# State-space layer of a two-layer diffusion backbone: the scaled x is split one or two chunks ahead of its state product, the decays begin four chunks ahead, and their tile is parted in two

## The chip, the core and the metric

The kernel runs on one core of a Trainium2 chip. TensorE (PE in the profile) multiplies matrices into accumulator banks (PSUM); VectorE (DVE), ScalarE (ACT) and GpSimd (POOL) work elementwise, POOL on the working memory (SBUF) alone; SyncE (SP) issues nearly all transfers (DMAs). Each engine works through its own queue in order and waits at the head of it. The metric is the time of one execution in microseconds (us) as the device gives it.

## The reference, cut to what matters

One inference step goes through an even layer and then an odd layer, for 128 context tokens and 1024 latent tokens, which makes nine chunks of 128 tokens; chunk 0 is the context. The odd layer (attention) is not touched. The even layer holds a bidirectional state-space scan (Mamba-2 SSD) beside a pooling branch. The scan has 16 heads of width 64 in 4 groups, state size 128, and for one direction it computes

```python
a = chunk(dt * A)                                  # dt > 0, A < 0
a_cs = jnp.cumsum(a, axis=2)
l_mat = exp(where(lower, a_cs[l] - a_cs[s], -inf)) # decay from token s to token l in a chunk
cb = einsum('bclgn,bcsgn->bcgls', Cc, Bc)
y_diag = einsum('bcgrls,bcsgrp->bclgrp', cb * l_mat, xdt)
decay_to_end = exp(a_cs[:, :, -1:] - a_cs)
states = einsum('bclgn,bclgr,bclgrp->bcgrpn', Bc, decay_to_end, xdt)
h = h * exp(a_cs[:, :, -1]) + states               # from chunk to chunk
y_off = einsum('bclgn,bcgrpn,bclgr->bclgrp', Cc, h_prev, exp(a_cs))
y = y_diag + y_off
```

The second direction does the same on the flipped sequence; both results and `x * D` are summed. The context's final state of each direction is an output too. Matrix products must be nearly as exact as in 32 bits.

## The kernel before, in words

A 32-bit operand of a matrix product is split in two 16-bit halves: ACT rounds it to the first (`split`, line 510), and POOL, or DVE where none is named, subtracts that from the operand to get the second (line 511). A product is then three matmuls (`mm3`, lines 330 to 332): high by high, high by low, low by high. Since these lines are a helper's, the profile tells products apart by their tiles: `xshl` is the split of the scaled x, `hb` and `hf` that of the backward and forward states, `E` the decays (and, later, the masked product), `psss` an accumulator bank of the state-space stage (four of them, taken in turn).

The scan runs group by group (`ssd_group`, `ssd_steps`, g = 0 to 3). For one group:

- Contexts (`context`, line 788): the state product of chunk 0 for both directions, scaled by ACT (line 791) and stored. In odd groups they come before the state pass, in even groups in the first step of the output pass.
- State pass (line 841): for one direction, chunk by chunk, the state before the chunk is split into `hb`, and seven steps carry it on. A step (`step`, line 775) takes x of the chunk in 32 bits (`x32`, line 758, the sum of its two halves, here on POOL), multiplies it on DVE by the decay to the chunk's end (line 767, tile `xs`, two buffers), splits it on ACT and POOL (tile `xshl`, two buffers), multiplies B by it on PE, and adds the product to the decayed state on DVE (line 780). The decayed state is made on POOL (line 778).
- Output pass (line 868): for each of the nine chunks, the other direction's state is carried along with the same step, here with x32 on DVE; `y` starts as x times the diagonal term on POOL (line 875); the masked product times x is added to it (lines 893 and 895), and the two states' part (lines 901 to 906).
- `decay(c)` (line 794) prepares the mask of a chunk, for both directions in one tile `E` of 1024 columns, five buffers (`NE`): a DMA brings the cumulated decays of both directions to all partitions (line 798, 512 KB); then for each of four heads ACT adds one bias (line 801), DVE takes the minimum with the other direction (line 802) and ACT writes the dt factors over the second half (line 804); an exponential on ACT (line 806) and a multiply on POOL (line 807) end it.
- `prep(c)` (line 812) multiplies B and C of the chunk on PE into a bank, takes the diagonal from it on DVE (lines 819 and 821), multiplies the mask by the bank on DVE (line 825), and splits the result on ACT and POOL. The two 16-bit halves, `M`, are written over the second half of the same tile, so that one buffer is held from the DMA to the output product.

In the text, decays of the first three chunks stand in steps 0, 2 and 4 of the state pass (`DECAY_AT`), preps of two in steps 5 and 6; in the output pass chunk n has the decay of chunk n + 3 and the prep of chunk n + 2.

PE's instructions keep the order of the text. Between the steps, `yield` hands the order to a filler (`Filler`, line 72), which puts in as many matmuls of projections and of the pooling branch as the yielded share says: `FILL` over the sum of shares (`STORE`, `OUT_A`, `OUT_B`, `CONTEXT`, `LEAD`) is the number of estimated microseconds for one share. The elementwise work of the filler (convolutions, gates, weight splits at lines 323 and 324) goes to the same queues. The order within the queues of DVE, ACT, POOL and SP isn't that of the text: a scheduler fixes it when the program is built, by priorities, by when its model has operands ready, and by when buffers are free. The scan's steps have the higher priority; the loads of weights (line 313) do too.

Of the kernel before, what the change touches and what calls it, by code (L numbers as in the profile page):

```python
# [10 lines left out]
F32 = mybir.dt.float32  # L11
F16 = mybir.dt.float16
I32 = mybir.dt.int32
AF = mybir.ActivationFunctionType
# [27 lines left out]
STORE, OUT_A, OUT_B, CONTEXT = 1.0, 0.5, 0.5, 0.75  # L42
DECAY_AT, PREP_AT = (0, 2, 4), (5, 6)
ADA_EVERY = 4.5
# [4 lines left out]
SCORE_BANKS = ("S1", "s4", "S1", "m3", "S1")  # L49
NE = 5  # L50

# [170 lines left out]
class Builder:  # L222
# [518 lines left out]
    def ssd_steps(self, g):  # L741
# [13 lines left out]
        def v3(x):  # L755
            return x.rearrange("p (a b) -> p a b", a=4)

        def x32(c, eng=nc.vector):
            x = self.wt([P, 256], F32, tag="x32", bufs=2)
            xk = self.xb[d1, c // 3][0]  # L760
            eng.tensor_tensor(x.rearrange("p (a b) -> p a b", a=2), xk[:, :, 0, c % 3], xk[:, :, 1, c % 3], ALU.add)
            return x

        def state(c, d, x):

            xs = self.wt([P, 256], F32, tag="xs", bufs=2)
            nc.vector.tensor_tensor(v3(xs), v3(x), hcol(self.dec, c, d), ALU.mult)
            hl = self.wt([P, 2, 256], F16, tag="xshl", bufs=2)
            self.split(hl, xs, nc.gpsimd)
            st = self.pt("ss")[:, :256]  # L770
            bk = self.xb[d1, c // 3][1]
            self.mm3(st, bk[:, 0, c % 3], bk[:, 1, c % 3], hl[:, 0], hl[:, 1], True, True)
            return st

        def step(h, c, d, x):

            hn = self.wt([P, 256], F32, tag="hst", bufs=2)
            nc.gpsimd.tensor_tensor(v3(hn), v3(h), hcol(self.etot, c, d), ALU.mult)
            st = state(c, d, x)
            nc.vector.scalar_tensor_tensor(hn, st, IWS, hn, ALU.mult, ALU.add)  # L780
            return hn
# [6 lines left out]
        def context(x, d):  # L788

            so = self.wt([P, 256], F32, tag="xs", bufs=2)  # L790
            nc.scalar.activation(so, state(0, d, x), AF.Copy, scale=IWS)
            nc.sync.dma_start(self.O["ssd"][d, :, g * 256:(g + 1) * 256], so)

        def decay(c):

            ef = self.wt([P, 1024], F32, tag="E", bufs=NE)
            E = ef.rearrange("p (a b c) -> p a b c", a=2, b=4)
            nc.sync.dma_start(ef, self.csrow[g, c].rearrange("d h l -> (d h l)").partition_broadcast(P))
            for hh in range(4):
                i = g * 4 + hh  # L800
                nc.scalar.activation(E[:, 0, hh], E[:, 0, hh], AF.Identity, bias=self.cs[:, c, i:i + 1])
                nc.vector.scalar_tensor_tensor(E[:, 0, hh], E[:, 1, hh], self.cs[:, c, 16 + i:17 + i], E[:, 0, hh],
                                               ALU.add, ALU.min)
                nc.scalar.activation(E[:, 1, hh], self.tri[:, 0], AF.Identity, bias=self.dt[:, c, 16 + i:17 + i],
                                     scale=self.dtd[:, c, i:i + 1])
            nc.scalar.activation(E[:, 0], E[:, 0], AF.Exp)
            nc.gpsimd.tensor_tensor(E[:, 0], E[:, 0], E[:, 1], ALU.mult)
            Es[c] = ef

        Es, dgs = {}, {}  # L810

        def prep(c):

            ef = Es.pop(c)
            cb = self.pt("ss")[:, :P]
# [7 lines left out]
            dgs[c] = dgt[:, 0:4]  # L823
            S = ef[:, :512].rearrange("p (a b) -> p a b", a=4)
            nc.vector.tensor_tensor(S, S, cb.rearrange("p (a b) -> p a b", a=1).broadcast_to([P, 4, P]), ALU.mult)
            M = ef[:, 512:].bitcast(F16).rearrange("p (x a b) -> p x a b", x=2, a=4)
            self.split(M, S, nc.gpsimd)
            return M

        yield LEAD[g]  # L830
        order = range(NCH) if d1 == 0 else range(NCH - 1, -1, -1)
# [7 lines left out]
        Ms = {}  # L839
        scan = range(1, 9) if d0 == 0 else range(8, 0, -1)  # L840
        for n, c in enumerate(scan):
            self.split(hb[:, c - 1], h, nc.gpsimd)
            if n == 7:
                break
            h = step(h, c, d0, x32(c, nc.gpsimd))
            if n in DECAY_AT:
# [16 lines left out]
        carry(scan[0], h)  # L863
        x = x32(order[0])
        if d1:
            h = step(h, scan[0], d1, x)
            carry(scan[1], h)
        for n, c in enumerate(order):
            if n + 3 < NCH:
                decay(order[n + 3])  # L870
            if n + 2 < NCH:
                Ms[order[n + 2]] = prep(order[n + 2])
            yield OUT_A

            nc.gpsimd.tensor_tensor(v3(y[:, c]), v3(x), dgs.pop(c).rearrange("p (a b) -> p a b", b=1).broadcast_to([P, 4, 64]),
                                    ALU.mult)
# [5 lines left out]
            if n + 1 < NCH:  # L882
                e = order[n + 1]
                x = x32(e)
                if e in scan[:7]:
                    h = step(h, e, d1, x)
                    carry(scan[scan.index(e) + 1], h)
# [754 lines left out]
```

## Time and profile before

| what | value |
|---|---|
| median of 3 runs | 2299.93 us (2294.38 to 2300.79) |
| the profiled execution | 2299.1 us |
| its span, first to last instruction | 2297.3 us |
| PE, DVE, ACT, POOL busy in the span | 2031.8, 1534.2, 1293.6, 1067.8 us |
| mean granted TensorE clock | 0.954 of full |
| loads of the decays (tile E) | 36, 512 KB each, 3.9 us to landing (median) |
| loads of even-layer weights (tile w from in_wev) | 40, 512 KB each, 4.0 us to landing (median) |

How its lines are read. In a table of waits, "A line <- B line: t, n, m" says that engine A stood idle t us in total, in n waits, of which the longest took m, before its instruction of that line, and that B's instruction ended those waits. In a row of a tile, the three numbers behind the count are the shortest, the median and the longest duration in nanoseconds, followed by the first and the last start in us. In a table of windows, each engine has its busy time and its number of instructions, and behind them stand the granted clock, the share of the DMA engines' time, and the rate in GB/s; a table of one line's instructions has that line's engine alone. Busy time includes time in which an instruction was held up after its start.

### The profile page before, as it was taken

What the parts mean: (1) busy time and instruction counts of PE and PEld (TensorE: products, weight loads), DVE (VectorE), ACT (ScalarE), POOL (GpSimd) and SP (SyncE); (2) the same over time, 40 slices, a digit from 0 to 9 for tenths busy, and PEclk for the clock granted to TensorE, in tenths of its full rate; (3) what the DMA queues carried; (4) which work ended last, traced back from release to release, by engine and by line L of the source; (5) the groups of instructions that cost most, each with busy time, mean ns of one, the idle gap of its engine ahead of it and who ended that gap; (6) DMA issues with size and microseconds to landing.
All of it is one profiled execution on the core that took longest, in us unless ns stands there. A gap on an engine that the chain in (4) does not pass through costs nothing. (4 is left out here: it accounts for less than half of the span.)

```text
span 2297.3 us, 50851 instructions
## 1 busy us (share of the span) xinstructions
PE 2031.8 (88%) x20258; PEld 1452.5 (63%) x20258; DVE 1534.2 (67%) x3329; ACT 1293.6 (56%) x3530; POOL 1067.8 (46%) x997
## 2 busy tenths in 40 slices
PE   4997788787999999978898998988977999898997
PEld 2654475564557555656686676775766777686566
DVE  5868989789585444747877777778785545552334
ACT  5575666666363311436666666666676777773321
POOL 1378677876674100134445445345345656552001
PEclk9998899998999999999999999999999999999999
DMA  7221514224657522135555455544556786899412
GB/s 275 70 80 50 147 58 111 82 80 131 222 184 209 174 71 86 40 102 114 97 125 115 96 113 116 105 107 105 105 124 133 151 168 143 171 180 205 155 47 83
DMA packets 434990, 283.17 MB, mean 123 GB/s; under 512 B 374432, under 2 KB 385216, under 8 KB 434752
## 3 DMA queue, kind: packets, MB, share of 16 engines
q1 hardware_dynamic: 433776, 279.34, 49.7%
q8 instruction: 158, 2.59, 0.5%
q10 hardware_dynamic: 976, 0.58, 0.1%
q14 instruction: 80, 0.66, 0.1%
HBM read 133.38 MB, written 29.05 MB: 71 GB/s over the span
## 5 line engine op out<-in xcount | busy, mean ns | idle before, releaser
L330 PE MATMUL psmm<-h,whl 128*128 128x384 f16 (+1 forms) x1104 | 369.9, 336 | 16.7 <-DVE q L1171 11.5
L331 PE MATMUL psmm<-h,whl 128*128 128x384 f16 (+1 forms) x1104 | 368.7, 335 | 2.3 <-DVE h L507 1.7
L332 PE MATMUL psmm<-h,whl 128*128 128x384 f16 (+1 forms) x1104 | 368.7, 335 | 0.0
L330 PE MATMUL psmm<-whl,h 128*128 128x128 f16 x1920 | 345.9, 224 | 0.0
L331 PE MATMUL psmm<-whl,h 128*128 128x128 f16 x1920 | 345.7, 224 | 0.0
L332 PE MATMUL psmm<-whl,h 128*128 128x128 f16 x1920 | 345.4, 224 | 0.0
L330 PEld LDWEIGHTS <-whl 128*128 128x128 f16 x2256 | 226.6, 100 | 162.0 <-issue 23.6
L332 PEld LDWEIGHTS <-whl 128*128 128x128 f16 x2256 | 225.4, 100 | 157.1 <-issue 18.6
L331 PEld LDWEIGHTS <-whl 128*128 128x128 f16 x2256 | 225.9, 100 | 151.6 <-issue 27.6
L1307 POOL TENSOR_TENSOR phl<-p,phl 128x1152 f16<-128x1152 f32 (+1 forms) x72 | 159.9, 2221 | 249.8 <-ACT phl L1306 210.2
L330 PEld LDWEIGHTS <-h 128*128 128x128 f16 x2520 | 250.9, 100 | 9.4 <-issue 3.8
L331 PEld LDWEIGHTS <-h 128*128 128x128 f16 x2520 | 250.8, 100 | 6.9 <-issue 1.2
L332 PEld LDWEIGHTS <-h 128*128 128x128 f16 x2520 | 250.8, 100 | 0.0
L324 DVE SCALAR_TENSOR_TENSOR whl<-w,whl 128x512 f16<-128x512 f32 x248 | 191.0, 790 | 67.6 <-ACT whl L323 67.1
L1385 POOL TENSOR_TENSOR phl<-p,phl 128x1024 f16<-128x1024 f32 (+2 forms) x72 | 135.0, 1876 | 117.6 <-ACT phl L1384 117.2
L323 ACT ACTIVATE whl<-w 128x512 f16<-128x512 f32 x248 | 140.6, 609 | 78.8 <-PE psmm L332 42.3
L1289 ACT ACTIVATE p<-psS,sms 128x384 f32<-128x384 f32 (+1 forms) x240 | 136.0, 569 | 66.0 <-DVE sms L1286 65.6
L1174 POOL TENSOR_TENSOR sw<-sw,sin 128x384 f32<-128x384 f32 (+1 forms) x78 | 87.4, 1121 | 154.2 <-DVE sw L1173 126.4
L1303 DVE SCALAR_TENSOR_TENSOR p<-p,sms,p 128x384 f32<-128x384 f32 (+1 forms) x200 | 151.9, 793 | 2.5
L1282 DVE TENSOR_REDUCE mx<-psS 128x1 f32<-128x384 f32 (+1 forms) x240 | 125.2, 540 | 37.4 <-PE psS L1280 37.4
L1280 PEld LDWEIGHTS <-Q 128*128 128x128 f16 x800 | 73.7, 98 | 117.6 <-issue 82.4
L504 POOL TENSOR_TENSOR h<-mt,h 128x384 f16<-128x384 f32 (+2 forms) x32 | 29.1, 919 | 252.8 <-ACT h L503 252.8
(396 smaller groups left out, 6122.8 us busy)
## 6 DMA issues: line engine op xcount, KB each, us to landing
w<-in_wod SPq DMA_DIRECT2D x52, 512.0 KB, 3.7
w<-in_wev SPq DMA_DIRECT2D x40, 512.0 KB, 4.0
E<-csrow SPq DMA_DIRECT2D x36, 512.0 KB, 3.9
Q<-qhl SPq DMA_DIRECT2D x64, 288.0 KB, 4.6
go_dr<-gl SPq DMA_DIRECT2D x15, 576.0 KB, 3.3
wada<-in_w_ada SPq DMA_DIRECT2D x32, 256.0 KB, 5.4
o<-in_w_ada SPq DMA_DIRECT2D x16, 512.0 KB, 5.8
xT<-in_w_ada SPq DMA_DIRECT2D x16, 512.0 KB, 6.5
```

Source lines behind the costliest of these rows:

```text
L323: nc.scalar.activation(hl[:, 0, a:e], w[:, a:e], AF.Copy if scale is None else AF.Identity, scale=sc)
L324: nc.vector.scalar_tensor_tensor(hl[:, 1, a:e], w[:, a:e], sc, hl[:, 0, a:e], ALU.mult, ALU.subtract)
L330: mm(out, ah, bh, start=start, stop=False)
L331: mm(out, ah, bl, start=False, stop=False)
L332: mm(out, al, bh, start=False, stop=stop)
L1174: nc.gpsimd.tensor_tensor(sw[:, o:], sw[:, o:], self.sinT[:, a:b], ALU.mult)
L1280: nc.tensor.matmul(sv, q[:, m, x, qs], k[:, m, o + c0:o + c1], start=x == 0, stop=x == 1)
L1282: nc.vector.tensor_reduce(out=mx[:, j:j + 1], in_=sv, axis=AX.X, op=ALU.max)
L1289: nc.scalar.activation(pm[:, c0:c1], ss[j], AF.Exp, bias=nb, accum_out=sm[:, i:i + 1])
L1303: nc.vector.scalar_tensor_tensor(p[0][:, c0:c1], p[1][:, c0:c1], sm[:, 2:3], p[0][:, c0:c1], ALU.mult, ALU.add)
L1307: nc.gpsimd.tensor_tensor(phl[:, w:2 * w], p[0][:, :w], phl[:, :w], ALU.subtract)
L1385: nc.gpsimd.tensor_tensor(phl[:, 2 * w:4 * w], p, phl[:, :2 * w], ALU.subtract)
```

## The change

- `state` is parted. `scaled(c, d, x)` does the scaling and the split and returns the halves; `state(c, hl)` does the product alone. `step` takes the halves.
- In the state pass, the first chunk's x is summed, scaled and split before the first yield of the group, and each further one ahead of the step before it. In the output pass, `ahead(n)` sums x of the n-th chunk of the order, and scales and splits it where that chunk has a state step; it is called for chunks 0 and 1 ahead of the loop, and for chunk n + 2 in chunk n, behind its prep.
- The contexts scale and split where they did.
- `x32` and `xshl` have three buffers instead of two; `xs` keeps two.
- The decay's tile becomes two tiles of 512 columns, each with its own DMA of half the size: `E0` (tag E, four buffers), which is free once prep has split it, and `E1` (tag EM, six buffers), which takes the second direction, then the dt factors, then the halves `M`. Together they take the room of the five before.
- Decays stand at steps 0, 2, 3 and 5 of the state pass, four instead of three, and in the output pass one chunk further ahead, n + 4.

The products on PE, their order, and the number of elementwise instructions are the same.

```diff
-DECAY_AT, PREP_AT = (0, 2, 4), (5, 6)
+DECAY_AT, PREP_AT = (0, 2, 3, 5), (5, 6)
...
-NE = 5
+NE0, NE1 = 4, 6
...
-            x = self.wt([P, 256], F32, tag="x32", bufs=2)
+            x = self.wt([P, 256], F32, tag="x32", bufs=3)
...
-        def state(c, d, x):
+        def scaled(c, d, x):
 
             xs = self.wt([P, 256], F32, tag="xs", bufs=2)
             nc.vector.tensor_tensor(v3(xs), v3(x), hcol(self.dec, c, d), ALU.mult)
-            hl = self.wt([P, 2, 256], F16, tag="xshl", bufs=2)
+            hl = self.wt([P, 2, 256], F16, tag="xshl", bufs=3)
             self.split(hl, xs, nc.gpsimd)
+            return hl
+
+        def state(c, hl):
+
             st = self.pt("ss")[:, :256]
...
-        def step(h, c, d, x):
+        def step(h, c, d, hl):
...
-            st = state(c, d, x)
+            st = state(c, hl)
...
-            nc.scalar.activation(so, state(0, d, x), AF.Copy, scale=IWS)
+            nc.scalar.activation(so, state(0, scaled(0, d, x)), AF.Copy, scale=IWS)
...
-            ef = self.wt([P, 1024], F32, tag="E", bufs=NE)
-            E = ef.rearrange("p (a b c) -> p a b c", a=2, b=4)
-            nc.sync.dma_start(ef, self.csrow[g, c].rearrange("d h l -> (d h l)").partition_broadcast(P))
+            E0 = self.wt([P, 4, P], F32, tag="E", bufs=NE0)
+            E1 = self.wt([P, 4, P], F32, tag="EM", bufs=NE1)
+            for d, E in enumerate((E0, E1)):
+                nc.sync.dma_start(E.rearrange("p h l -> p (h l)"),
+                                  self.csrow[g, c, d].rearrange("h l -> (h l)").partition_broadcast(P))
...
-            S = ef[:, :512].rearrange("p (a b) -> p a b", a=4)
-            M = ef[:, 512:].bitcast(F16).rearrange("p (x a b) -> p x a b", x=2, a=4)
+            M = E1.rearrange("p a b -> p (a b)").bitcast(F16).rearrange("p (x a b) -> p x a b", x=2, a=4)
...
+        scan = range(1, 9) if d0 == 0 else range(8, 0, -1)
+        nxt = scaled(scan[0], d0, x32(scan[0], nc.gpsimd))
         yield LEAD[g]
...
-            h = step(h, c, d0, x32(c, nc.gpsimd))
+            hl = nxt
+            if n < 6:
+                nxt = scaled(scan[n + 1], d0, x32(scan[n + 1], nc.gpsimd))
+            h = step(h, c, d0, hl)
...
-        x = x32(order[0])
+        xs, hls = {}, {}
+
+        def ahead(n):
+
+            if n < NCH:
+                c = order[n]
+                xs[c] = x32(c)
+                if c in scan[:7]:
+                    hls[c] = scaled(c, d1, xs[c])
+
+        ahead(0)
+        ahead(1)
         if d1:
-            h = step(h, scan[0], d1, x)
+            h = step(h, scan[0], d1, hls.pop(scan[0]))
             carry(scan[1], h)
         for n, c in enumerate(order):
-            if n + 3 < NCH:
-                decay(order[n + 3])
+            if n + 4 < NCH:
+                decay(order[n + 4])
             if n + 2 < NCH:
                 Ms[order[n + 2]] = prep(order[n + 2])
+            ahead(n + 2)
             yield OUT_A
 
+            x = xs.pop(c)
...
-                x = x32(e)
-                if e in scan[:7]:
-                    h = step(h, e, d1, x)
+                if e in hls:
+                    h = step(h, e, d1, hls.pop(e))
                     carry(scan[scan.index(e) + 1], h)
```

More of the change, by code (lines that the diff above doesn't have):

```diff
@@ L790, in context @@
             so = self.wt([P, 256], F32, tag="xs", bufs=2)
-            nc.scalar.activation(so, state(0, d, x), AF.Copy, scale=IWS)
+            nc.scalar.activation(so, state(0, scaled(0, d, x)), AF.Copy, scale=IWS)
             nc.sync.dma_start(self.O["ssd"][d, :, g * 256:(g + 1) * 256], so)
         def decay(c):
-            ef = self.wt([P, 1024], F32, tag="E", bufs=NE)
-            E = ef.rearrange("p (a b c) -> p a b c", a=2, b=4)
-            nc.sync.dma_start(ef, self.csrow[g, c].rearrange("d h l -> (d h l)").partition_broadcast(P))
+            E0 = self.wt([P, 4, P], F32, tag="E", bufs=NE0)
[3 more added lines that the diff above has]
+                                  self.csrow[g, c, d].rearrange("h l -> (h l)").partition_broadcast(P))
             for hh in range(4):
                 i = g * 4 + hh
-                nc.scalar.activation(E[:, 0, hh], E[:, 0, hh], AF.Identity, bias=self.cs[:, c, i:i + 1])
-                nc.vector.scalar_tensor_tensor(E[:, 0, hh], E[:, 1, hh], self.cs[:, c, 16 + i:17 + i], E[:, 0, hh],
+                nc.scalar.activation(E0[:, hh], E0[:, hh], AF.Identity, bias=self.cs[:, c, i:i + 1])
+                nc.vector.scalar_tensor_tensor(E0[:, hh], E1[:, hh], self.cs[:, c, 16 + i:17 + i], E0[:, hh],
                                                ALU.add, ALU.min)
-                nc.scalar.activation(E[:, 1, hh], self.tri[:, 0], AF.Identity, bias=self.dt[:, c, 16 + i:17 + i],
+                nc.scalar.activation(E1[:, hh], self.tri[:, 0], AF.Identity, bias=self.dt[:, c, 16 + i:17 + i],
                                      scale=self.dtd[:, c, i:i + 1])
-            nc.scalar.activation(E[:, 0], E[:, 0], AF.Exp)
-            nc.gpsimd.tensor_tensor(E[:, 0], E[:, 0], E[:, 1], ALU.mult)
-            Es[c] = ef
+            nc.scalar.activation(E0, E0, AF.Exp)
+            nc.gpsimd.tensor_tensor(E0, E0, E1, ALU.mult)
+            Es[c] = E0, E1
         Es, dgs = {}, {}
         def prep(c):
-            ef = Es.pop(c)
+            S, E1 = Es.pop(c)
             cb = self.pt("ss")[:, :P]
@@ L839, in ssd_steps @@
         Ms = {}
-        scan = range(1, 9) if d0 == 0 else range(8, 0, -1)
         for n, c in enumerate(scan):
```

## The prediction

> **What bounds the kernel now.** I read the page first: the span and the engines' busy time.
>
> ```profile
> span 2297.3 us, 50851 instructions
> ...
> PE 2031.8 (88%) x20258; PEld 1452.5 (63%) x20258; DVE 1534.2 (67%) x3329; ACT 1293.6 (56%) x3530; POOL 1067.8 (46%) x997
> ```
>
> TensorE (PE) is busy for 88% of the span and VectorE (DVE) for 67%. The change touches only the state-space stage, about 130 to 712 us, so I cut that by windows. The eight rows are, for each of the four groups, the state pass (seven state steps) and the output pass (nine chunks); I set the borders by eye, from where the state products and the first output products start.
>
> ```profile
> core 0: us, PE busy (x) PEld busy (x) DVE busy (x) ACT busy (x) POOL busy (x), PEclk, DMA share, GB/s
> 130.00:190.00 60.00, 51.44 (x318) 31.08 (x316) 43.25 (x59) 39.81 (x98) 47.13 (x57) 0.97 0.22 72
> 190.00:275.00 85.00, 61.81 (x436) 37.84 (x436) 78.09 (x132) 50.35 (x123) 63.75 (x77) 0.84 0.36 99
> 275.00:330.00 55.00, 50.33 (x560) 38.87 (x557) 45.57 (x67) 35.74 (x98) 40.37 (x50) 0.97 0.40 103
> 330.00:410.00 80.00, 66.12 (x535) 43.68 (x533) 72.65 (x128) 49.36 (x130) 63.48 (x71) 0.91 0.36 95
> 410.00:475.00 65.00, 53.58 (x622) 41.97 (x620) 51.88 (x73) 41.08 (x121) 54.66 (x85) 0.92 0.24 67
> 475.00:565.00 90.00, 72.14 (x499) 44.48 (x498) 81.10 (x142) 57.51 (x140) 60.62 (x65) 0.89 0.39 115
> 565.00:640.00 75.00, 69.58 (x712) 46.04 (x710) 43.41 (x72) 36.89 (x105) 50.43 (x77) 0.98 0.59 196
> 640.00:712.00 72.00, 66.44 (x539) 38.49 (x537) 56.32 (x130) 41.10 (x104) 46.70 (x57) 0.95 0.55 187
> ```
>
> PE is the limit in the state passes: 51.44 us of 60, 50.33 of 55, 53.58 of 65, 69.58 of 75. In the first three output passes DVE is: 78.09 of 85, 72.65 of 80, 81.10 of 90, about 91%. So a wait of PE taken away in a state pass should come back as time, while in an output pass only what also relieves DVE, or lets it idle less, comes back. Next I asked what PE waits for between 130 and 712 us.
>
> ```profile
> PE psss L330 <- ACT xshl L510: 27.4, 6, 10.4
> PE psss L330 <- DVE E L825: 25.0, 11, 4.4
> PE psss L331 <- POOL xshl L511: 18.9, 12, 3.0
> ```
>
> The tile xshl is the split of the scaled x, in two halves: ACT makes the first, POOL the second. PE stands 27.4 + 18.9 = 46.3 us for it. The other large wait, 25.0 us, ends with line 825, DVE's multiply in prep, which frees an accumulator bank.
>
> **Which of the 46.3 us the change covers.** Not all are state steps. The two context products of a group stay where they are, without a lead. PE's waits there, in the windows 175 to 206, 275 to 290 and 474 to 488 us:
>
> ```profile
> PE psss L330 <- ACT xshl L510: 10.4, 1, 10.4
> PE psss L331 <- POOL xshl L511: 4.5, 2, 2.9
> ```
>
> ```profile
> PE psss L330 <- ACT xshl L510: 1.8, 1, 1.8
> ```
>
> ```profile
> PE psss L331 <- POOL xshl L511: 3.0, 1, 3.0
> PE psss L330 <- ACT xshl L510: 2.5, 1, 2.5
> ```
>
> They sum to 22.2 us. Two waits on ACT's half lie in output passes, in the windows 350 to 355 and 650 to 656 us:
>
> ```profile
> PE psss L330 <- ACT xshl L510: 3.2, 1, 3.2
> ```
>
> ```profile
> PE psss L330 <- ACT xshl L510: 3.0, 1, 3.0
> ```
>
> The largest of a state pass lies between 430 and 442 us:
>
> ```profile
> PE psss L330 <- ACT xshl L510: 6.4, 1, 6.4
> PE psss L331 <- POOL xshl L511: 1.7, 1, 1.7
> ```
>
> So 3.2 + 3.0 = 6.2 us are covered in output passes, and the rest, 46.3 - 22.2 - 6.2 = 17.9 us, in state passes. The rows of the tile xshl's chain, of its product in the window 410 to 430 us, and of DVE's own waits between 130 and 712 us:
>
> ```profile
> L767 DVE TENSOR_TENSOR xs<-x,dec x64: 407/820/2364, 117.5 to 667.8; 128x256 f32<-128x256 f32 x64
> L510 ACT ACTIVATE xshl<-xs x64: 394/404/422, 118.4 to 676.4; 128x256 f16<-128x256 f32 x64
> L511 POOL TENSOR_TENSOR xshl<-xs,xshl x64: 659/671/1830, 120.3 to 679.4; 128x256 f16<-128x256 f32 x64
> ```
>
> ```profile
> L330 PE MATMUL psss<-xshl,bk x2: 273/273/273, 418.6 to 423.8; 128*128 128x256 f16 x2
> ```
>
> ```profile
> DVE xs L767 <- POOL xshl L511: 34.6, 22, 5.8
> ...
> DVE x L761 <- POOL y L875: 8.6, 10, 2.1
> ```
>
> **State pass.** No work is added: 28 steps scale, split and multiply as before, but scaling and splitting are written one step earlier, with a third buffer for x and for xshl. The chain is 0.82 + 0.40 + 0.67 = 1.9 us by its medians, so what made it late was the place in the queues. Two products stand 423.8 - 418.6 = 5.2 us apart; that lead covers every wait except the one of 6.4 + 1.7 = 8.1 us, of which 2.9 would remain. That gives at most 17.9 - 2.9 = 15 us, at least nothing (rival 1). I take three quarters, 11 us, because a PE that runs earlier asks everything else earlier.
>
> **Output pass, the split x.** Two chunks of lead cover all of the 6.2 us, but those passes belong to DVE: I take half, 3 us, between 0 and 6.2. The third x32 buffer also loosens DVE's wait at line 761, which ended each time with the POOL multiply that reads the old x: 8.6 us of DVE idle, of which I take 2, between 0 and all.
>
> **Decays.** Each chunk's decay is the same work in two tiles. The rows are line 802 in the window 190 to 275 us, and the loads:
>
> ```profile
> 190.00:275.00 85.00, 13.22 (x24) 0.84 0.36 99
> ```
>
> ```profile
> L798 SPq DMA_DIRECT2D E<-csrow x36: 319/423/1533, 132.5 to 676.0; - x36
> ```
>
> Four line-802 instructions make a decay: 13.22 / 24 x 4 = 2.2 us of DVE. Before, the buffers let five decays run ahead of a group, into the output pass before it; then one starts as each output chunk frees its tile. After, the E tile has four buffers and is free once prep has split, while the masked product lives on in the other tile. So four run ahead, two fall into the state pass, three are left for the output pass: two decays, 4.4 us of DVE, leave each of the three full output passes, 13.2 us in all. DVE has room for them in the state passes (43.25 of 60 and the like). What they return lies between 0 and 13.2 us. I take 4, because no row shows DVE idle for the decay's product at line 825: the multiply was late by its place in DVE's queue, not for want of its input, so an earlier decay itself frees nothing.
>
> **The clock.** Windows around two waits:
>
> ```profile
> 150.00:157.50 7.50, 5.09 (x33) 3.08 (x32) 6.30 (x11) 7.14 (x20) 5.76 (x9) 1.00 0.00 1
> 157.50:160.90 3.40, 3.40 (x13) 1.57 (x12) 3.39 (x5) 1.09 (x3) 2.84 (x6) 0.50 0.50 158
> ...
> 191.70:205.30 13.60, 4.59 (x16) 2.12 (x15) 13.33 (x14) 5.84 (x14) 13.60 (x14) 0.50 0.18 58
> ...
> 434.00:444.20 10.20, 4.37 (x15) 2.12 (x15) 7.99 (x13) 8.70 (x26) 10.20 (x24) 0.50 0.27 47
> ```
>
> After waits the clock stands at 0.50. From 191.7 to 205.3 us PE idles 9.0 us, and its 4.59 us of work at half rate lost 2.3: a quarter of a microsecond for each idle one. The 11 + 3 + 4 = 18 us of waits taken out return 4.5 us. From 150 to 157.5 us PE idled only 7.50 - 5.09 = 2.41 us, and the clock halved all the same. [...]
>
> **What it costs.** In the even groups the contexts come after two splits made ahead have taken two of the three xshl buffers, so the second context's split has to wait for the first context's product. Hidden, it costs 0; at worst a wait like today's 10.4 + 2.9 = 13.3 us returns in each of two groups; I take 3, near nothing, because filler matmuls stand between the two products. The loads become 72 of half the size: 36 more issues of 0.42 us, 15.2 us of SyncE's queue, with weight loads behind them. Between a little below 0 (a half may land sooner than the whole) and 15.2, I take 1, as the table of waits has no PE wait on a weight load.
>
> Line 767 takes from 407 to 2364 ns for one shape; I read that as DVE standing against POOL, which is busy 47.13 us of 60 in the first state pass, and keep the median. [...]
>
> **Sum.** 11 + 3 + 2 + 4 + 4.5 - 3 - 1 = 20.5 us less. The profiled execution took 2299.1 us (1.8 us around its span), 0.8 below the median of three, 2299.93. So 2299.1 - 20.5 = 2278.6, rounded to 2279.
>
> **Rival 1, no change (0.19).** The scaling already runs ahead. Its rows say so: line 767 starts at 117.5 us and line 330 at 131.6, and the last at 667.8 and 690.0.
>
> ```profile
> L330 PE MATMUL psss<-xshl,bk x64: 269/273/373, 131.6 to 690.0; 128*128 128x256 f16 x64
> ```
>
> Engines other than PE are ordered by the scheduler, not by the text, so writing it earlier may move little. Then the 11, 3 and their clock go, the decays' 4 and 2 stay against a cost of 4: 2299.1 - 2 = 2297. Against it: the waits are there although the text has the chain just ahead of the product, and two buffers limit the lead.
>
> **Rival 2, slower (0.18).** The xs tile keeps two buffers. DVE already idles 34.6 us in 22 waits before line 767, 1.57 us each, until POOL has split the older one. Scaling written ahead puts line 767 in front of the state's add, the bank-freeing multiply and the evictions; everything behind it on DVE stands too. If each of the 21 output-pass steps of the three full passes waits 1.57 us, that is 33 us on the limiting engine. Less 11 in the state passes, 4 for decays and 4 for their clock, it is 14 slower: 2313. It decides where that idle time passes about 55 us (34.6 plus what the gains pay). For it: waits on this buffer are the longest of DVE's. Against it: few now fall into output passes, as DVE is 91% busy there.
>
> **Rival 3, much faster (0.09).** With lighter output passes the context waits vanish as well: 22.2 x 1.25 = 28 us beside the 20.5 and without their 3: 2299.1 - 51.5 = 2248. Against it: no line of the change gives contexts a lead.
>
> **Numbers.** The forecast has 0.54; its own range is 2262 to 2291, from its terms nearly full to a third. A measurement of this kernel can tell about 0.3% (6.9 us) from no change. Faster: the forecast and rival 3, 0.63; same: rival 1, 0.19; slower: rival 2, 0.18. The range for 8 in 10 goes from 2252, which leaves half of rival 3 out, to 2308, which leaves out most of rival 2, spread around 2313.
>
> **What would show it.** Right: PE's waits on xshl fall from 46.3 to about 30 us, mostly contexts; the state passes' clock rises above 0.92 to 0.97; line 802 counts fall from 24 in an output pass by about eight. Wrong: PE's waits on line 825 or on the state's add grow by what xshl lost (rival 1), DVE's idle time before line 767 grows past 55 us (rival 2), or a context wait is over 13.3 us.

## The result, and the profile after

| kernel | median | runs | ratio to before, 95% interval |
|---|---|---|---|
| before | 2300.36 us | 2294.38 to 2302.58 | 1 |
| after | 2331.01 us | 2329.62 to 2333.32 | 1.0138 [1.0117, 1.0159] |

The change made the kernel slower by 1.4%, about 31 us, against a forecast of 20 us faster. The profiled execution of after took 2333.32 us. First its page, span and busy time.

```profile
span 2331.5 us, 50933 instructions
...
PE 2041.1 (88%) x20258; PEld 1455.5 (62%) x20258; DVE 1527.2 (66%) x3329; ACT 1295.0 (56%) x3530; POOL 1050.3 (45%) x997
```

The instructions of PE, DVE, ACT and POOL are the same in number. Of the 34.2 us between the two spans (2331.5 and 2297.3), 9.3 are longer busy time of PE (2041.1 and 2031.8) and the rest is time in which it stands. Where it was lost is seen by setting the same PE instruction of both traces side by side, since the order on PE did not change. The first matmuls of the 64 state products start later than before by:

```
start before (us)  131.6  170.2  214.0  293.0  320.6  371.5  418.6  465.2  533.5  602-644  654.7  690.0
later after (us)     1.4    4.7    5.4    8.3    8.3   11.5   23.9   16.8   30.1  18.9-21.3  21.5   30.2
```

Nearly all of the loss is made inside this stage, and most of it in its output passes: from 320.6 to 418.6, from 465.2 to 533.5 (11 us of which come back by 602), and from 654.7 us on. In the first state pass the delay grows by 3.3 us (131.6 to 170.2); in the later ones it stays as it is (293.0 to 320.6) or shrinks (418.6 to 465.2). The windows of the three full output passes, cut as in the prediction, for after:

```profile
190.00:275.00 85.00, 61.23 (x398) 36.58 (x398) 67.71 (x126) 52.86 (x127) 61.64 (x71) 0.84 0.33 89
...
330.00:410.00 80.00, 58.13 (x531) 40.59 (x529) 65.17 (x120) 49.33 (x131) 51.69 (x60) 0.87 0.28 82
...
475.00:565.00 90.00, 69.36 (x564) 45.75 (x562) 69.96 (x130) 57.30 (x151) 60.10 (x67) 0.89 0.26 78
```

Before, DVE was busy for 78.09, 72.65 and 81.10 us of the three full output passes; now for 67.71, 65.17 and 69.96. Much of that fall is only the cut, since after runs up to 30 us late and the same times hold other work. Cut at the same PE instructions instead (those that start next after each border in before), DVE is busy for 70.7, 72.6 and 81.1 us before, and 65.7, 80.5 and 71.5 after. It was not relieved: over the stage it does nearly as much (482 and 477 us) and stands more. Between one and the same pair of PE instructions (the 700th and the 5000th, about the whole stage) DVE idles 150.9 us after and 116.3 before, ACT 266.5 and 238.7, PE 113.5 and 90.6. All three stand longer, by 23 to 35 us, and none is full.

What PE, ACT and DVE wait for between 130 and 745 us; first those rows of before that the prediction did not show:

```profile
ACT E L801 <- DMA E<-csrow: 22.2, 12, 4.6
...
DVE E L802 <- ACT E L801: 5.8, 9, 1.6
...
PE psss L330 <- DVE hst L780: 4.2, 5, 2.3
...
PE psss L330 <- DVE y L906: 1.2, 2, 1.0
```

and after (the lines behind 767 moved: 780 is now 784, 798 is 803, 801 is 807, 802 is 808, 804 is 810, 825 is 830, 875 is 897, 895 is 916, 906 is 927):

```profile
ACT E L807 <- DMA E<-csrow: 60.7, 23, 6.5
DVE xs L767 <- POOL xshl L511: 42.4, 24, 4.6
...
PE psss L330 <- ACT xshl L510: 21.2, 5, 6.7
DVE E L808 <- ACT E L807: 21.0, 14, 4.9
PE psss L330 <- DVE E L830: 20.8, 9, 6.6
PE psss L330 <- DVE hst L784: 20.7, 8, 9.2
...
PE psss L330 <- DVE y L927: 12.4, 8, 3.3
...
PE psss L330 <- DVE y L916: 10.2, 5, 6.0
...
DVE E L808 <- DMA EM<-csrow: 9.1, 3, 4.7
...
PE psss L331 <- POOL xshl L511: 4.9, 5, 3.0
```

PE's waits on the scaled x did fall, from 46.3 to 21.2 + 4.9 = 26.1 us, and all that is left are the contexts': in the state steps and output passes none remains. But PE's waits on DVE grew by more: for the state's add, line 784, 20.7 us for 4.2 before, and for the output, lines 916 and 927, 22.6 us for 1.8. DVE itself was late, and so were its suppliers: of the 34.6 us by which it idles longer, 24.3 lie at the decays' line 808 (21.0 + 9.1 us, for 5.8 before), behind a load or behind ACT's step that had waited for one. The largest row is new in its size: ACT stands 60.7 us for a decay's load, nearly three times the 22.2 of before. SP's queue shows where the load itself was held, before and after:

```profile
SPq L798 <- PE psss L332: 32.2, 10, 7.1
```

```profile
SPq L803 <- POOL EM L511: 155.0, 28, 14.8
```

Before, a decay's load waited for an output product (PE) to free the tile. Now it waits for POOL's half of a prep's split. One case, from the timeline of after, on POOL, SP and ACT (start, duration, engine, line; idle time before it in brackets):

```profile
334.84 2.28 POOL L511 TENSOR_TENSOR EM<-E,EM 128x512 f16<-128x512 f32 x1
...
342.29 0.67 POOL L511 TENSOR_TENSOR xshl<-xs,xshl 128x256 f16<-128x256 f32 x1 [3.42 <-ACT xshl L510]
```

```profile
337.15 0.33 SPq L803 DMA_DIRECT2D E<-csrow  x1
```

```profile
340.63 1.28 ACT L807 ACTIVATE E<-E,cs 128x128 f32<-128x128 f32 x4 [2.98 <-DMA E<-csrow]
341.81 0.40 ACT L510 ACTIVATE xshl<-xs 128x256 f16<-128x256 f32 x1
```

The split ends at 337.12 us, the load goes out at 337.15 and lands at 340.6. The decay's first step is ACT's next instruction and holds ACT for 2.98 us; behind it stands the split of a scaled x, which the scan needs and whose input DVE had finished at 330.84 us, and behind that POOL. In this one case PE had other work: its product with that split starts at 343.24 us without a wait. Nothing needs this decay soon: in after, the product that ends a decay (line 813) is finished 14 us or more ahead of the multiply that uses it (line 830), with a median of 28.7 us.

### The profile page after: what moved, and what is told of

The parts are those of the page before. It is cut to its first block, busy times and chain, and to the rows that moved or that the text cites. A ratio compares the mean times of both kernels' runs of the same rounds, so it can differ in the third digit from the quotient of the medians.

```text
span 2331.5 us, 50933 instructions
## 1 busy us (share of the span) xinstructions
PE 2041.1 (88%) x20258; PEld 1455.5 (62%) x20258; DVE 1527.2 (66%) x3329; ACT 1295.0 (56%) x3530; POOL 1050.3 (45%) x997
## 5 line engine op out<-in xcount | busy, mean ns | idle before, releaser
L324 DVE SCALAR_TENSOR_TENSOR whl<-w,whl 128x512 f16<-128x512 f32 (+1 forms) x248 | 191.1, 792 | 63.1 <-ACT whl L323 62.6
```

The lines of the kernel that those rows point to most:

```text
L324: nc.vector.scalar_tensor_tensor(hl[:, 1, a:e], w[:, a:e], sc, hl[:, 0, a:e], ALU.mult, ALU.subtract)
```

## The experiments

Each ran beside the kernel before; ratios are to it. After the two traces, the theory was that the decays' parted tile costs, by its loads or its lifetimes; the rivals were the scaled x made ahead and, later, any new order of the queues, too few buffers, and SP's queue. The expectations name and number them as they were held at the time.

**Parts of the change.** Kernel `look`: scaled x ahead, with the old tile and decays. `look_state`: that in the state pass alone. `tiles`: parted tile 4/6 and the earlier decays, without scaled x ahead. `e5m5`: the whole change with five buffers for each half.

```diff
look (from after; decay and prep as before):
-DECAY_AT, PREP_AT = (0, 2, 3, 5), (5, 6)
+DECAY_AT, PREP_AT = (0, 2, 4), (5, 6)
-NE0, NE1 = 4, 6
+NE = 5
...
-                decay(order[n + 4])
+                decay(order[n + 3])
look_state (from look):
-        ahead(0)
-        ahead(1)
+        x = x32(order[0])
...
-                    h = step(h, e, d1, hls.pop(e))
+                    h = step(h, e, d1, scaled(e, d1, x))
tiles (from before; decay and prep as after):
-DECAY_AT, PREP_AT = (0, 2, 4), (5, 6)
+DECAY_AT, PREP_AT = (0, 2, 3, 5), (5, 6)
-NE = 5
+NE0, NE1 = 4, 6
...
-                decay(order[n + 3])
+                decay(order[n + 4])
e5m5 (from after):
-NE0, NE1 = 4, 6
+NE0, NE1 = 5, 5
```

> Only the scaled x made ahead (x and its split with three buffers), decays and their tile as before the change. Theory 1, that the loss of 31 us comes from the decays' tile (its first half has four buffers, each freed only when prep has split it, so that loads go out at the last moment and ACT and DVE stand in their queues for the landing): faster than before by 10 to 25 us, ratio 0.989 to 0.996, ACT's wait on the E loads near 22 us. Theory 2, that scaling ahead puts DVE and POOL work in front of what frees banks: slower by 20 to 40 us, ratio 1.009 to 1.017.

> Only the scaled x of the state pass made one step ahead (with the third buffers), the output pass's as before the change, decays as before. Theory 1: faster by 5 to 15 us, ratio 0.993 to 0.998. Theory 2, if it lies in the output pass: the same; the difference between this run and the one with both lookaheads is what the output pass's lookahead costs, 20 to 40 us.

> Only the tile parted in two (four and six buffers) and the decays a chunk earlier; the scaled x as before the change. Theory 1: slower by 30 us or more, ratio 1.013 to 1.025, ACT's wait on the E loads about 60 us as with the whole change. Theory 2: within 0.3% of before, or faster by up to 10 us.

> The whole change with five buffers for each half of the decays' tile in place of four and six (the same room). Theory 1: the first half's loads go out a chunk earlier, ACT's wait on them falls from 60.7 to about 30 us, and the time falls by 15 to 35 us from 2331, ratio to before 0.998 to 1.007. Theory 2: the ratio stays at 1.010 to 1.016.

Measured: look 1.0038 [1.0023, 1.0053], look_state 1.0039 [1.0026, 1.0052], tiles 1.0167 [1.0150, 1.0184], e5m5 1.0120 [1.0098, 1.0142]. The scaled x made ahead does not gain anything, it costs 0.4%, and all of that is there with the state pass alone. The large loss comes with the decays' tile, and a fifth buffer for its first half helps little.

**Parts of the tile part.** `two_loads`: the kernel before, its one tile loaded by two half loads. `decay4`: the kernel before with the decays one chunk earlier. `part55`: the kernel before with the parted tile 5/5. `hold`: the whole change, with a decay's steps written later than its loads, and queued on ACT behind the split that then stands before them.

```diff
two_loads (from before):
-            nc.sync.dma_start(ef, self.csrow[g, c].rearrange("d h l -> (d h l)").partition_broadcast(P))
+            for d in range(2):
+                nc.sync.dma_start(ef[:, d * 512:(d + 1) * 512],
+                                  self.csrow[g, c, d].rearrange("h l -> (h l)").partition_broadcast(P))
decay4 (from before):
-DECAY_AT, PREP_AT = (0, 2, 4), (5, 6)
+DECAY_AT, PREP_AT = (0, 2, 3, 5), (5, 6)
...
-                decay(order[n + 3])
+                decay(order[n + 4])
part55 (from before; decay and prep as after):
-NE = 5
+NE0, NE1 = 5, 5
hold (from after):
+            self.behind = self.split(M, S, nc.gpsimd)
...
+                with self.tc.issue_after(self.behind):
+                    self.held.popleft()()
```

> The kernel before with one edit: the decays' tile is loaded by two DMAs of half the size; tile, buffers, decays and x as before. Theory 1b, that the scheduler queues ACT's first bias right at the landing it reckons for the smaller load, so that ACT stands at the head of its queue until the load has really landed: ACT's wait on the E loads rises from 22 to 40 us or more, the bias follows its load's issue by a median near 3.5 us in place of 6.1, and the time is 10 to 30 us longer, ratio 1.004 to 1.013. Theory 1a, that the buffers' lifetimes (four for the first half) make the loads late: within 0.3% of before.

> The kernel before with the decays one chunk earlier in the text (steps 0, 2, 3 and 5, chunk n + 4), one tile of five buffers. Theories 1a and 1b: within 0.4% of before, since five buffers already bound how far decays run ahead; ACT's wait on the E loads stays near 22 us. Rival: the earlier text itself costs, 20 us or more.

> The kernel before with the tile parted in two of five buffers each, decays and x as before. Theory 1b: like the tile with two loads, ACT's wait on the E loads 45 to 60 us, ratio 1.006 to 1.015. Theory 1a: within 0.4% of before, since no lifetime is shorter of buffers than before.

> The whole change, with the decays' ACT work queued behind the ACT split that stands ahead of it in the text (in the state pass that of the state, in the output pass that of the prep), while the loads go out as early as before. Theory 1b: ACT's wait on the E loads falls from 60.7 to under 15 us and most of the loss returns: 15 to 40 us less than 2331, ratio 0.997 to 1.007. Theory 1a, or if what stands in the queues is not the wait on the load: the ratio stays above 1.010.

Measured: two_loads 1.0058 [1.0038, 1.0078], decay4 1.0015 [1.0004, 1.0025], part55 1.0131 [1.0114, 1.0148], hold 1.0100 [1.0081, 1.0119]. Two small loads for a large one cost 0.6%, as theory 1b had it, but ACT's wait for the loads is 26.8 us, not the 40 or more by which 1b explained it. The earlier decays cost next to nothing; the parted tile alone, with as many buffers as before and nothing earlier, costs what the whole change costs. Waits of `part55`, and of its SP queue:

```profile
ACT EM L806 <- DVE E L804: 54.9, 32, 8.1
ACT E L803 <- DMA E<-csrow: 41.4, 21, 4.4
PE psss L330 <- ACT xshl L510: 39.8, 7, 9.3
...
PE psss L330 <- DVE hst L780: 12.1, 7, 3.2
DVE E L804 <- DMA EM<-csrow: 11.2, 7, 3.0
```

```profile
SPq L799 <- POOL EM L511: 128.4, 24, 10.9
```

The first half, free after the split, was loaded 8 to 35 us ahead of the second, which waits for an output product; DVE then stands for the second half too. In `hold` the stand at the load is gone, but the time is not back:

```profile
ACT EM L817 <- DVE E L815: 56.6, 53, 3.9
...
ACT EM L511 <- DVE E L842: 35.6, 20, 4.1
...
ACT E L814 <- DMA E<-csrow: 6.1, 1, 6.1
```

ACT stood 54.6 us less for loads, and the kernel won 9 us, for the steps now stood for DVE. So ACT's wait for the load is not the price by itself.

**Both loads together.** In `paired55` (from part55) and `after_paired` (from the whole change) the first half's load is queued behind the second's. `after_onetile` is the whole change with the old tile. `bufs3` is the kernel before with a third buffer for x32 and xshl: a control for whether any new order of the queues costs.

```diff
paired55 (from part55), after_paired (from after):
-            for d, E in enumerate((E0, E1)):
-                nc.sync.dma_start(E.rearrange("p h l -> p (h l)"), ...)
+            late = nc.sync.dma_start(E1.rearrange("p h l -> p (h l)"), ...)
+            with self.tc.issue_after(late.ins):
+                nc.sync.dma_start(E0.rearrange("p h l -> p (h l)"), ...)
after_onetile (from after; decay and prep as before):
-NE0, NE1 = 4, 6
+NE = 5
bufs3 (from before):
-            x = self.wt([P, 256], F32, tag="x32", bufs=2)
+            x = self.wt([P, 256], F32, tag="x32", bufs=3)
-            hl = self.wt([P, 2, 256], F16, tag="xshl", bufs=2)
+            hl = self.wt([P, 2, 256], F16, tag="xshl", bufs=3)
```

> The kernel before with the decay's tile parted 5/5 and the old decay times, as in the run part55 (ratio 1.0131), but the second direction's load is written first and the first direction's load is queued behind it, so that both halves go out together although the first half's buffer is free earlier. Theory 2a (the parted tile costs because its first half is asked for as soon as its buffer is free, 12 to 35 us ahead of the second, and the decay's steps then stand half ready at the heads of ACT's and DVE's queues): ratio near the run with one tile and two loads, 1.004 to 1.008; ACT's waits for a decay's load fall from 41.4 us to under 30, DVE's wait for the second half from 11.2 us to under 4. Theory 2b (any new order of the queues costs, whatever its cause): ratio stays at 1.011 or over, with ACT's waits lower or not.

> The whole change (buffers 4 and 6), with the first half's load queued behind the second half's, so that the two go out together. Theory 2a: ratio to before falls from 1.0138 to between 1.004 and 1.009, and ACT's waits for a decay's load from 60.7 us to under 35. Theory 2b: stays at 1.011 or over. Between them the two causes share.

> The whole change with the decay's tile left as before (one tile, one load, five buffers): scaled x ahead in both passes and the decays one chunk earlier. If the parted tile is what costs (2a): the sum of its parts, 1.0038 and 1.0015, so 1.003 to 1.007, and ACT's waits for a decay's load at 20 to 27 us. If the lookahead and the earlier decays hurt each other without the parted tile: 1.010 or over.

> The kernel before with a third buffer for x32 and xshl and nothing else: no work, no load and no line of the text moved, only more freedom for the order of the queues (DVE's order differs in hundreds of places). Theory 2b (any new order costs): 1.003 or over. Theory 2a has no loss in it: 0.998 to 1.002; DVE's wait for x32 (8.6 us before) should go to about 0, and the prediction's 2 us for it should show here alone.

Measured: paired55 0.9995 [0.9981, 1.0009], after_paired 1.0076 [1.0053, 1.0100], after_onetile 1.0016 [1.0005, 1.0028], bufs3 0.9991 [0.9976, 1.0006]. after_paired's ratio is in its range, but ACT still waits 52.7 us for loads, where under 35 was expected. Four answers. The order of the two loads alone decides over part55's 1.3%. The whole change with one tile costs 0.2%, so the parted tile is 1.2 of its 1.4%. A new order of the queues by itself need not cost anything. And bufs3 shows what a wait on the scaled x is worth; its PE waits:

```profile
PE psss L330 <- ACT xshl L510: 12.8, 3, 5.9
...
PE psss L331 <- POOL xshl L511: 10.4, 5, 4.6
```

The 46.3 us fell to 12.8 + 10.4 = 23.2, by more than the forecast's fall to about 30, and the time stayed within 0.3% of before; PE's waits for the output's line 895 grew from 0.6 to 12.3 us. Of paired55, the waits and SP's queue:

```profile
ACT EM L808 <- DVE E L806: 38.0, 38, 3.3
...
ACT E L805 <- DMA E<-csrow: 28.0, 14, 4.7
...
PE psss L330 <- ACT xshl L510: 23.9, 7, 12.1
...
PE psss L330 <- DVE hst L780: 2.6, 5, 0.7
```

```profile
SPq L798 <- PE psss L332: 33.7, 10, 5.8
```

The load waits for an output product again, ACT's stand is 28.0 us for 41.4 in part55, its wait for DVE's minimum 38.0 for 54.9, and DVE's wait for the second half is gone. The texts of the two kernels differ in nothing but the loads' order, so they also show where the time went: ACT stands 30.3 us longer at a decay's steps in part55 (96.3 for 66.0), PE 15.9 us longer for ACT's split of the scaled x, and 9.5 for the state's add, while PE's idle time between its 700th and 5000th instruction is 116.1 us for 91.3.

**Why only half came back in the whole change.** `e5m5_paired` is after_paired with five buffers for each half; `part46_paired` is paired55 with four and six; `paired55_b3` is paired55 with bufs3's buffers.

```diff
e5m5_paired (from after_paired):
-NE0, NE1 = 4, 6
+NE0, NE1 = 5, 5
part46_paired (from paired55):
-NE0, NE1 = 5, 5
+NE0, NE1 = 4, 6
paired55_b3 (from paired55):
-            x = self.wt([P, 256], F32, tag="x32", bufs=2)
+            x = self.wt([P, 256], F32, tag="x32", bufs=3)
-            hl = self.wt([P, 2, 256], F16, tag="xshl", bufs=2)
+            hl = self.wt([P, 2, 256], F16, tag="xshl", bufs=3)
```

> The whole change, with five buffers for both halves (the run e5m5 gave 1.0120) and the first half's load queued behind the second half's. Both loads of a chunk then go out when an output product frees the second half, not when a prep's split frees the first. Theory 3a (what costs is the first half's load going out at the end of a prep's split, or long ahead of the other half): ratio 1.000 to 1.004, near the whole change with one tile (1.0016), ACT's waits for a decay's load under 32 us. Theory 3b (parting the tile costs beside the lookahead whatever the order of the loads): 1.007 or over.

> The kernel before with the tile parted 4/6, decays at the old places, scaled x as before, and the first half's load queued behind the second half's. It differs from the run paired55 (0.9995) in the buffers alone: with four, the first half's load waits for a prep's split again. Theory 3a: slower than paired55, 1.004 to 1.010, ACT's waits for a decay's load over 40 us. Theory 3c (the 0.8 per cent left in the run after_paired come from the earlier decays and the lookahead, not from the four buffers): 0.998 to 1.003.

> The run paired55 (0.9995) with the third buffer for x32 and xshl of the run bufs3 (0.9991): a version that might beat the kernel before. If both small changes add: 0.996 to 0.999. If PE's waits that they remove are replaced by others, as in bufs3, where PE's waits on xshl halved and the time stayed: 0.999 to 1.002.

Measured: e5m5_paired 1.0054 [1.0038, 1.0070], part46_paired 1.0129 [1.0111, 1.0146], paired55_b3 1.0022 [1.0012, 1.0032]. With four and six buffers the pairing doesn't help (the expected range ended at 1.010): it is the first half's buffer that a load waits for. From part46_paired:

```profile
ACT E L805 <- DMA E<-csrow: 60.2, 25, 4.7
```

```profile
SPq L801 <- POOL EM L511: 97.3, 22, 12.6
```

e5m5_paired came out over its range. The third kernel doesn't beat the kernel before, though each of its two edits by itself cost nothing.

**Number of buffers, or moment of the load.** `e4` is the kernel before with four buffers for its one tile; `part45_paired` is paired55 with four and five.

```diff
e4 (from before):
-NE = 5
+NE = 4
part45_paired (from paired55):
-NE0, NE1 = 5, 5
+NE0, NE1 = 4, 5
```

> The kernel before, one tile and one load, with four buffers for the decay's tile instead of five and nothing else. Theory 4a (four buffers cost in the run part46_paired because the first half is then freed, and its load sent, at the end of a prep's split, while ACT is about to be free; in this run the output product still frees the tile): 0.998 to 1.004, ACT's waits for a decay's load under 32 us. Theory 4b (four buffers cost because too few decays run ahead): 1.008 or over; for it the decays would have to be needed soon after they end, while in the profile of before the product of a decay ends 7 us or more ahead of the multiply that uses it.

> The run paired55 (0.9995) with four buffers for the first half and five, as there, for the second; part46_paired (1.0129) had six for the second. Theory 4a: as slow as part46_paired, 1.008 to 1.015, ACT's waits for a decay's load over 45 us. If it was the sixth buffer of the second half, whose loads then go out 50 to 80 us ahead of the first half's in each group: 0.998 to 1.004.

Measured: e4 0.9983 [0.9970, 0.9997], part45_paired 1.0038 [1.0019, 1.0057]. Fewer decays ahead cost nothing. What I expected of part45_paired by theory 4a was wrong: I took it that the first half's load would go out at a split there. The ratio is in the range given for the other case, that the sixth buffer matters, and its SP queue shows why:

```profile
SPq L798 <- PE psss L332: 40.1, 12, 7.2
...
SPq L801 <- POOL EM L511: 3.4, 3, 1.8
```

With five buffers the second half is the one that is waited for, and the first follows it. So the sixth buffer of the second half is what lets the split decide. Counted in the traces, the loads of the first half (of 36) that go out in the half microsecond after the end of a prep's split on POOL:

| kernel | first-half loads at a split's end | ACT's wait for loads, us | ratio |
|---|---|---|---|
| e4 | 1 | 19.9 | 0.9983 |
| paired55 | 1 | 28.0 | 0.9995 |
| before | 0 | 22.2 | 1 |
| after_onetile | 2 | 23.8 | 1.0016 |
| part45_paired | 6 | 35.2 | 1.0038 |
| e5m5_paired | 0 | 36.3 | 1.0054 |
| after_paired | 25 | 52.7 | 1.0076 |
| hold | 30 | 6.1 | 1.0100 |
| e5m5 | 27 | 57.0 | 1.0120 |
| part46_paired | 25 | 60.2 | 1.0129 |
| part55 | 28 | 41.4 | 1.0131 |
| after | 31 | 60.7 | 1.0138 |
| tiles | 32 | 62.3 | 1.0167 |

The six other kernels so far have at most 2 such loads and ratios from 0.9991 to 1.0058. So every kernel here with 25 or more loads at a split costs over 0.7%, every other one under 0.6%, though the nearest two (after_paired and two_loads) overlap in their intervals. The number doesn't set the size: with 25 to 32 such loads the cost goes from 0.8 to 1.7%.

**Which queue pays.** `pool_loads` is the whole change with the decays' loads issued by POOL, so that SP doesn't stand at them.

```diff
pool_loads (from after):
-                nc.sync.dma_start(E.rearrange("p h l -> p (h l)"),
+                nc.gpsimd.dma_start(E.rearrange("p h l -> p (h l)"),
```

> The whole change with the decay's loads issued by POOL instead of SP. The moment of the load stays: the first half's buffer is freed by POOL's own split. Theory 5a (the loss comes from ACT and DVE standing at steps of a decay whose load went out at the end of a prep's split): no gain, 1.009 or over, ACT's waits for a decay's load still over 45 us. Theory 5b (it comes from SP, which stands 155.0 us in 28 waits for such a split with weight loads queued behind it): 1.005 or under. What an issue costs POOL isn't known from the runs so far; a result over 1.0138 would contain it.

Measured: 1.0277 [1.0256, 1.0299], 2362.29 us. Its waits on a load, and the two issues on POOL:

```profile
ACT E L807 <- DMA E<-csrow: 73.5, 26, 6.2
```

```profile
L803 POOL DMA_DIRECT2D E<-csrow x36: 536/577/710, 126.7 to 722.3; - x36
L803 POOL DMA_DIRECT2D EM<-csrow x36: 536/553/600, 135.0 to 723.5; - x36
```

Taking SP's 155.0 us of standing away returned nothing; ACT's stand grew. The 72 issues take 36 x 0.577 + 36 x 0.553 = 40.7 us of POOL, enough to cover the added 31 us, so this run alone can't exclude a gain beneath it. The trace of after speaks against SP's queue more plainly: no instruction of the stage waits for a load of even-layer weights (tile w), and between PE's 700th and 5000th instruction the waits of PE, DVE, ACT and POOL for loads and stores other than the decays' sum to 8.3 us there, for 20.6 before.

## Why the prediction was wrong

**The step that failed** is the decays' term. It took "free once prep has split it" as a gain only: "two decays, 4.4 us of DVE, leave each of the three full output passes", worth between 0 and 13.2 us. Neither half holds. The decays did not leave; line 802 in the three full output passes of before, and line 808 in those of after:

```profile
190.00:275.00 85.00, 13.22 (x24) 0.84 0.36 99
330.00:410.00 80.00, 11.90 (x21) 0.91 0.36 95
475.00:565.00 90.00, 13.44 (x28) 0.89 0.39 115
```

```profile
190.00:275.00 85.00, 12.16 (x28) 0.84 0.33 89
330.00:410.00 80.00, 11.13 (x24) 0.87 0.28 82
475.00:565.00 90.00, 9.50 (x26) 0.89 0.26 78
```

They went from 24, 21 and 28 to 28, 24 and 26, not down by eight each. Cut at the same PE instructions, as above, they rose to 25, 32 and 31, and in the state passes ahead of the second, third and fourth output pass they fell from 12, 15 and 8 to 4, 5 and 4: decays moved into the output passes instead of out of them. The buffers freed by each prep's split let the next decay, the next group's among them, start at once in the same pass. And parting the lifetimes moved the moment of the load from an output product to a prep's split. I had no term for that. The tile part measured alone is 1.0167 on the kernel before, and 1.2% of the whole change by difference, about 28 us of loss where I had 4 of gain. That "no row shows DVE idle for the decay's product" was right, and should have led further: work that is never late gains nothing from an earlier start, so the term's lower end had to lie below nothing.

**The state pass, -11, and the split x in the output pass, -3.** The mechanism came as forecast: waits on the split x fell by 20.2 us to 26.1 (about 30 forecast, mostly contexts'), and contexts' are all that is left. Its value didn't. bufs3 removed 23.1 us of them for no time at all, and look, with the lead, cost 0.4%. The sentence that fails is "a wait of PE taken away in a state pass should come back as time": PE gains within the pass and then stands for DVE in the next output pass, as the growing waits on lines 784, 916 and 927 show. They grow without the parted tile too: in look the waits on the split x fall by 18.0 us and those for the state's add and the output grow by 17.2 (23.2 for 6.0). This is the sign that rival 1 named, and what it said of the 11 and the 3, though not for its reason, that the scaling already ran ahead; it gave 2297, 7 us under the change with one tile (2304.41 us).

**The x32 buffer, -2.** Not seen: in bufs3 DVE's wait at line 761 is 8.0 us (8.6 before), and 13.4 in after. The third buffer was used up by the order: in bufs3 eight of the nine waits end with the same POOL multiply as before, and last as long to within 3 ns, but it is the next sum in DVE's queue that stands there.

**The clock, -4.5.** It went the other way, as the waits did. Between the 700th and the 5000th instruction of PE, which idles there for 90.6 us before and 113.5 after, the clock stands at 0.50 for 91.5 us before and 105.4 after; the windows from 330 to 410 us show 0.91 and 0.87. PE's busy time in that stretch rises with it, from about 507 to 513.5 us. The prediction's rate, a quarter of a microsecond for each idle one, would give 23 x 0.25 = 6 us for the 23 us by which PE idles longer; that agrees.

**Costs, +3 and +1.** The loads were to cost 1 us between a little below 0 and 15.2, as SP issues. Two half loads into one tile cost 0.6%, 13 us (two_loads), near the upper end. But the issues are not the price: paired55 sends the same 72 half loads and costs nothing. By what way two_loads loses is open: no instruction waits for a load of tile w there either, and ACT's wait for decays rose by 4.6 us only (26.8). The contexts' waits on the split x rose from 22.8 (the prediction's windows gave 22.2) to 26.1 us, by 3.3 where 3 were forecast; the longest on ACT's half is 6.7, not over the 13.3 us allowed.

**Rival 2** had the right sign, and 2313, but not by its mechanism. DVE's idle time before line 767 went from 34.6 to 42.4 us and never reached the 55 at which it decides. The lookahead did not put DVE into that stand; look costs 0.4%, not 14 us net. Nor did line 767 take longer at its new places; its durations are, in after,

```profile
L767 DVE TENSOR_TENSOR xs<-x,dec x64: 410/732/1497, 118.8 to 684.1; 128x256 f32<-128x256 f32 x64
```

a median of 732 ns for 820, and a longest of 1497 for 2364. The two traces agree with the prediction's reading, that DVE stands against POOL, as far as they go: with POOL idle all through, the line took 407 to 426 ns before (15 of 64) and 410 to 427 ns after (17), and each time that it took over 500 ns (37 before, 34 after) POOL was busy for at least 65% of it. But 5 and 4 of those under 430 ns ran wholly beside POOL's work, so whether POOL is what holds the line up is not shown.

**What is shown and what is not.** Shown: the loss is in the parted tile; it goes with loads that are sent when a prep's split frees the first half; putting the load back to an output product, by the order of two lines and by buffer counts, takes all of it away where nothing else is changed. Refuted: too few buffers (e4), a new order as such (bufs3), the smaller loads as such (paired55), the earlier place of the decays as such (decay4). Against SP's queue as the payer stands the trace of after, in which the waits for other loads fell; pool_loads alone doesn't settle it. Shown in part: how the early load turns into time. In part55 against paired55 ACT stands longer at a decay's steps, and PE for the split and the state's add that come late behind them; in after DVE's added idle time is mostly at the decays' line 808. Argued only: that this is the whole of the 28 us. hold, which took the stand at the load away, returned 9 us and made other stands. The scheduler that fixes the order puts a decay's step where its model has the load landed; what that model reckons is not shown here. Also open: between 0.2 and 0.5% in look, e5m5_paired and paired55_b3, whose parts don't add, and why after_paired (1.0076) is faster than part46_paired (1.0129) with the same 25 loads at a split.

No kernel here beats the kernel before by more than the 0.3% that can be told: e4, one buffer fewer, is the fastest at 2297.09 us against 2299.12.

## What to carry to other kernels

Parting a tile in two lifetimes changes which instruction sets its next load free. Ask, for each buffer, which event frees it, what the engines are doing at that moment, and which instruction is queued directly behind the load; an earlier start for work that already ends well ahead of its use gained nothing here and put its steps at the head of queues, where ACT stood 60.7 us for a decay's load instead of 22.2. A wait of PE in a table is worth time only when nothing behind it would be late instead: remove it by the cheapest means first, here a buffer count (23.1 us of waits gone, the time within 0.3%), and see whether the time moves. When you compare two profiles in windows, cut both at the same instructions: at the same times, a kernel that runs late shows other work.

## What the runs showed of the hardware

A load of half the size didn't land much sooner here. The pages list issues, size, and median us from issue to landing; before, then two_loads:

```profile
E<-csrow SPq DMA_DIRECT2D x36, 512.0 KB, 3.9
```

```profile
E<-csrow SPq DMA_DIRECT2D x72, 256.0 KB, 4.3
```

The halves, written one behind the other, took 4.3 us each where the whole took 3.9. In after, where 27 of the 36 pairs, taken in order, go out more than 2 us apart, they took 3.4 and 3.7:

```profile
E<-csrow SPq DMA_DIRECT2D x36, 256.0 KB, 3.4
EM<-csrow SPq DMA_DIRECT2D x36, 256.0 KB, 3.7
```
